# Interleaving a group's last down products with the next pair's first products, with the short weight loads on SyncE's queue, a third short buffer and subtraction for the quads' s4

## The chip, the cores and the metric

The kernel runs on one core of one Trainium2 chip. A core has TensorE (PE; its weight loads are shown as PEld), VectorE (DVE), ScalarE (ACT), GpSimd (POOL), SyncE (SP) and 16 DMA engines. The metric is the device time of one execution in microseconds (us); lower is better. The median of several runs is what counts.

## The reference

A two-layer encoder trunk on 512 tokens plus 16 meta tokens (T = 528 columns, 1024 features, float32). Each layer is a SwiGLU feed-forward net (FFN), a mixer (gated linear attention beside softmax attention) and a second FFN, each with its own RMS norm, added to the residual stream h. The change touches only the FFNs, of which there are four:

```python
def swiglu(x, w_gate, w_up, w_down):
    return (jax.nn.silu(x @ w_gate) * (x @ w_up)) @ w_down
...
    for l in range(DEPTH):
        h = h + 0.5 * swiglu(rmsnorm(h, norm_gains[l, 0]), ...)
        h = h + mixer(rmsnorm(h, norm_gains[l, 1]), ...)
        h = h + 0.5 * swiglu(rmsnorm(h, norm_gains[l, 2]), ...)
    return rmsnorm(h, final_norm)[:, N_META:]
```

The hidden width is 2816, that is 22 tiles of 128.

## The kernel before, in words

**Seven products in place of eight.** Weights and activations are split as 2x2 blocks and multiplied by the scheme of Strassen and Winograd: seven block products and a number of sums, instead of eight products. The products are called "1" to "7" in the code. Products "1", "2" and "4" take a block of the weights as it is (`DIRECT`, L50). "7", "6", "5" and "3" take sums of blocks, called s3, s2, s1 and s4: s3 = w21 - w11, s2 = w22 + s3, s1 = w21 + w22, s4 = s2 - w12.

**Steps of an FFN.** `ffn_steps` (L53) writes the order out by hand. The 22 hidden tiles are 11 pairs; a pair's gate and up weights give seven products, steps ("P", pair, product), done in `product_of_pair` (L549; its matmuls are L566). The pairs fall into groups of 4, 4 and 3 (`GROUPS`, L42). The first two groups are "fast" (`FAST`): their down product is done with the seven-product scheme too, in two halves (0 and 1) of the output rows, steps ("S", group, half, product, part), done in `fast_down` (L663; its matmuls are L680, its adds into h are L688). One such group of seven products of one half is called a quad here. The third group's down product is done plainly, steps "D". Steps "O" make the operands of the fast down product (L630 to L652).

Every step of kind P, and every S step in one piece, is 24 matmuls over 264 columns, or 256 in the last FFN, where the meta tokens are dropped. At a fast group's end the down products come in the order of `zip(AB, "16273465734")` (L75), where `AB` (L48) says which half: half 1's "1", half 0's "6", half 1's "2", half 0's "7", "3", "4", and then half 1's "6", "5", "7", "3", "4". The next group begins with its first pair's "1", "2", "6", "5" (L61, L64).

**Banks.** The results lie in two PSUM pools of two buffers each, "ss" and "s2"; even pairs use s2, odd pairs ss. The last pair of a fast group is odd (3 or 7). Half 1's "1", "6", "7" and "4" sum up in one buffer of ss; after "1", "6" and "7" VectorE adds what is there so far into h (L688) before the next product sums on. Half 1's "5" and "3" share another buffer of ss.

**Weights.** The class `Weights` (L166) loads each block of 128x1024 values (512 KB), and `make` (L245) splits it into two parts for TensorE: a rounded high part on ScalarE (whi, L259) and the low rest on VectorE (wlo, L260). `fetch` (L231) runs up to nine loads ahead, `make` two to three. Buffers:

- raw, 3: the blocks "11", "12" and "22" of the direct products, loaded on SyncE's queue (L193).
- long (`wsa`), 3: s3 and s4.
- short (`wsb`), 2: s2 and s1. Their plain loads go out on POOL's queue (L193, since `pool` is set).
- whi and wlo, 4 each.

`sums` (L205) makes the sums: s3 as a negation of w11 on ScalarE (L198) and an accumulating DMA of w21 (s<-win, L203); s2 as a plain load of w22 and an accumulating DMA of s3 (w<-s, L203); s1 as a plain load of w21 and an accumulating DMA of w22 (w<-win, L203). Accumulating DMAs are issued by POOL alone. s4 is made in one of two ways. For a "late" index (L219: pairs 2 to 10) it is a subtraction on VectorE (L228), s2 minus the kept w12, traced when "6" is made; w12 keeps its raw buffer until then. For the others (pairs 0 and 1, and the quads, which have the indices 11 to 14) it is a negation of w12 on ScalarE and an accumulating DMA of s2 (s<-w), traced when "2" is made.

**Order on the engines.** The program is written as one sequence of operations. A scheduler of the language then fixes the order on each engine and each queue before the run, by priorities and its own estimates of durations; it may move an instruction ahead of others whose inputs it expects later. At run time each engine and queue works through its own list.

The pools `wsa` and `wsb` are opened in `block_pools` (L1091).

Of the kernel before, what the change touches and what calls it, by code (L numbers as in the profile page):

```python
# [17 lines left out]
P = 128  # L18
# [24 lines left out]
FAST = 2  # L43
# [4 lines left out]
AB = (1, 0, 1, 0, 0, 0, 1, 1, 1, 1, 1)  # L48
# [4 lines left out]
def ffn_steps(opening):  # L53

    steps, pair = [], 0
    for g, n in enumerate(GROUPS):

        ahead = g == 0  # L60
        steps += [("P", p, c) for p in range(pair, pair + 1 + ahead) for c in "12"]  # L61
        early4 = (0, 1) if opening and ahead else ()
        steps += [("P", p, "4") for p in early4]
        steps += [("P", pair, c) for c in "65"]  # L64
        for i in range(n):
            p, more = pair + i, i + 1 < n
            early = [[("P", p + 1, "1")], [("P", p + 1, "2")]] if more else \
                [[("D", g, 0, 0, 2 * n - 2)], [("D", g, 1, 0, 2 * n - 2)]]
            if ahead and i == 0:
                early = [[], []]  # L70
            if not more and g < FAST:
                rest = [("S", g, 0, c, 2) for c in "125"]
                steps += [("O", g, 0), ("P", p, "7"), ("P", p, "4"), ("S", g, 0, "1", 1), ("P", p, "3")]
                steps += [("S", g, 0, c, 1) for c in "25"] + [("O", g, 1)] + rest
                steps += [("S", g, *t, 3) for t in zip(AB, "16273465734")]  # L75
                continue
            steps += early[0] + [("P", p, "7")] + early[1] + [("P", p, c) for c in "43" if c == "3" or p not in early4]
            if more:
                steps += [("P", p + 1, "6"), ("P", p + 1, "5")]
        if g >= FAST:  # L80
            steps += [("D", g, m, 0, 2 * n - 2) for m in range(2, HELD)]
            steps += [("D", g, m, 2 * n - 2, 2 * n) for m in range(HELD)]
            steps += [("D", g, m, 0, 2 * n) for m in range(HELD, KC)]
        pair += n
    return steps


def weight_plan():
# [8 lines left out]
    def ffn(l, f):  # L97
        for step in ffn_steps((l, f) == (0, 0)):
            if step[0] == "P":
                plan.append(("op", (l, f)) + step[1:])  # L100
            elif step[0] == "S":
                if step[4] != 2:
                    plan.append(("op", (l, f), NPAIR + QUADS * step[1] + step[2], step[3]))
            elif step[0] == "D":
                _, g, m, first, last = step
                mat("ffn_w_down", (l, f), m * P, 2 * sum(GROUPS[:g]) + first, last - first)
# [37 lines left out]
NPAIR = FF // P // 2  # L144
# [21 lines left out]
class Weights:  # L166
# [21 lines left out]
    def block(self, f, i, name, pool=None, tag="raw"):  # L188

        w = (pool or self.raw).tile([P, SLAB], F32, tag=tag, name=f"w{name}_{f[0]}{f[1]}_{i}")  # L190
        first = f + (i, name) == (0, 0, 0, "11")
        for a in np.split(np.arange(SLAB), 2 if first else 1):
            (self.nc.gpsimd if pool else self.nc.sync).dma_start(w[:, a[0] : a[-1] + 1], self.dram(f, i, name)[:, a[0] : a[-1] + 1])  # L193
        return w

    def negative(self, f, i, name, w):
# [8 lines left out]
    def sums(self, f, i, product, w):  # L205


        got = self.summed
        if product == "1":
            s3 = self.negative(f, i, "s3", w)  # L210
            self.add(s3, self.dram(f, i, "21"))
            s2 = self.block(f, i, "22", self.short, "wsb")
            self.add(s2, s3)
            got[f, i, "7"], got[f, i, "6"] = s3, s2
        if product == "12"[(f, i) in OPENING]:
            s1 = self.block(f, i, "21", self.short, "wsb")
            self.add(s1, self.dram(f, i, "22"))
            got[f, i, "5"] = s1
        late = 2 <= i < NPAIR  # L219
        if product == "2" and not late:  # L220
            s4 = self.negative(f, i, "s4", w)
            self.add(s4, got[f, i, "6"])
            got[f, i, "3"] = s4
        if product == "2" and late:
            self.kept = w
        if product == "6" and late:
            s4 = self.long.tile([P, SLAB], F32, tag="wsa", name=f"s4_{f[0]}{f[1]}_{i}")
            self.nc.vector.tensor_tensor(s4, w, self.kept, ALU.subtract)  # L228
            got[f, i, "3"] = s4
# [67 lines left out]
def build(tc, ctx, xt, wts, win, par, w2, const, umask, out):  # L297
    nc = tc.nc
    V, S, G, TE = nc.vector, nc.scalar, nc.gpsimd, nc.tensor
# [15 lines left out]
    def open_pools(side, psum=(), **bufs):  # L315
        made[0] += 1
        out = {}
        for n, b in bufs.items():
            space = dict(space=bass.MemoryType.PSUM) if n in psum else dict(side=side)
            out[n] = tc.alloc_tile_pool(name=f"{n}_{made[0]}", bufs=b, reuse_waits="tile", **space)  # L320
        slots.update(out)
        return out
# [218 lines left out]
    def ffn(l, f, norm, done, following):  # L541

        x, rs, up, n = norm.x, None, None, live[0]
        w = n // 2
        pools = open_pools("left", psum=("s2",), c=4, s2=2)
        made, hid, sums, raw, sets = {}, {}, {}, {}, {}
        risen = iter(range(KC))

# [144 lines left out]
        def down(g, m, first, last):  # L693
# [16 lines left out]
            if g == len(GROUPS) - 1:  # L710
                lower_h(m, rs)
                (done or finish_chunk)(m)

        steps = ffn_steps((l, f) == (0, 0))
        last_op = max(i for i, t in enumerate(steps) if t[0] == "P")
        for i, step in enumerate(steps):
# [372 lines left out]
        norm.pools = open_pools("right", **{"x": dict(x=16), "xc": dict(xc=8)}[kind])  # L1089

    def block_pools():  # L1091
        pools = open_pools("left", wsa=3, wsb=2)
        W.long, W.short = pools["wsa"], pools["wsb"]
        return pools

# [89 lines left out]
    def finish_chunk(c):  # L1185
        fin.square(c)
        gain(c, slice(0, SEQ))

    def ending(sums, operand, rs):

        table("abs_reciprocal_sqrt_and_small")
# [44 lines left out]
    first = Norm(G_NORM)  # L1236
    operand_pools(first, "xc")
    bp = [block_pools()]
    nc.sync.dma_start(h(1), xt[:, 1])
    first.pair(0)  # L1240
# [15 lines left out]
    for l in range(DEPTH):  # L1256
        a, b, c = norms[3 * l : 3 * l + 3]
        ffn(l, 0, a, b.chunk, lambda: operand_pools(b, "x"))
        close_pools(bp.pop())
        mixer(l, b, c.chunk_of_pair, lambda: (operand_pools(c, "xc"), bp.append(block_pools())))  # L1260
        if l < DEPTH - 1:
            d = norms[3 * l + 3]
            ffn(l, 1, c, d.pair_of, lambda: operand_pools(d, "xc"))
        else:
            ffn(l, 1, c, None, lambda: None)
# [72 lines left out]
```

## Time and profile before

| | |
|---|---|
| median of 3 runs | 2267.75 us (2262.52 to 2270.09) |
| the profiled execution's own time | 2280.39 us |
| its span, first to last instruction | 2278.6 us |
| mean granted TensorE clock | 0.989 |
| TensorE busy | 2188.9 us |
| VectorE, ScalarE, GpSimd busy | 1685.8, 1262.7, 246.1 us |
| moved by DMA | 338.68 MB |

How it is read: busy times of the engines overlap. A row of the grouped views gives the line of the code, the engine, the operation, output and inputs by the program's names (w, s and raw are weight blocks, ss and s2 PSUM buffers, both shown as ss; c and g hold activations), the count, the busy time and mean, and the idle time just before with what ended it. In a timeline row the first number is the start in us from the span's start, the second the duration; an entry in brackets is the idle time of that engine just before, and what ended it. Views of windows give, for a stretch of time, the busy time of each engine, the mean granted clock (PEclk, 1.00 is full), the mean busy share of the 16 DMA engines and the GB/s moved.

### The profile page before, as it was taken

To read this page: it belongs to the slowest core of one execution; us is meant where nothing else is said; L and a number is where in the kernel's file an instruction comes from. 1 tells how busy PE (TensorE), PEld (TensorE's weight loads), DVE (VectorE), ACT (ScalarE), POOL (GpSimd) and SP (SyncE) were. 2 spreads that over 40 slices of the span, in tenths; PEclk is the share of its full clock that TensorE was granted. 3 is DMA by queue.
4 is the path that set the end of the run, shared out by engine and by line. 5 is a ranking of instruction groups with operands and counts; after the bars stand their busy time and mean duration, and the time that the engine had idled before them with its cause. 6 is when DMAs were issued, how large, how long until landed. Compare 5 with 4: busy or idle time off the path is not lost.

```text
span 2278.6 us, 40100 instructions
## 1 busy us (share of the span) xinstructions
PE 2188.9 (96%) x16506; PEld 2088.3 (92%) x16506; DVE 1685.8 (74%) x2607; ACT 1262.7 (55%) x1831; POOL 246.1 (11%) x328
## 2 busy tenths in 40 slices
PE   6989999999999999999999899999999999999998
PEld 6989999989999999998999898998888888999997
DVE  7776867586886678667788768575878767786867
ACT  7545545354785565454575455454547846555553
POOL 1211110000000011111012111100000001121110
PEclk9999999999999999999999999999999999999999
DMA  8877873212113477777668777832121135887871
GB/s 241 217 198 185 203 195 106 77 54 66 47 38 112 129 189 187 204 192 202 175 148 208 201 193 178 201 114 86 56 74 47 47 121 136 216 213 213 204 204 65
DMA packets 94951, 338.68 MB, mean 149 GB/s; under 512 B 10544, under 2 KB 12976, under 8 KB 94768
## 3 DMA queue, kind: packets, MB, share of 16 engines
q0 software_dynamic: 46656, 169.89, 33.9%
q1 hardware_dynamic: 46160, 163.73, 21.2%
q8 instruction: 130, 2.13, 0.4%
q10 hardware_dynamic: 1952, 2.50, 0.3%
q14 instruction: 53, 0.43, 0.1%
HBM read 289.94 MB, written 2.10 MB: 128 GB/s over the span
## 4 chain that ended last, share of the span: by engine, by line
PE 60%; DMA 13%; DVE 12%; issue 8%; ACT 6%; POOL 1%; SPq 0%; DVEq 0%; POOLq 0%; ACTq 0%
PE ss L566 24%; PE mm L433 14%; DMA w<-win 10%; PE ss L433 9%; PE ss L680 4%; DVE wlo L260 3%; PE sm L433 2%; DMA w<-s 2%; ACT whi L259 1%; PE sm L1041 1%; DMA s<-w 1%; PE ss L1016 1%; POOL w L203 1%; ACT s L198 1%; PE sm L1057 1%
## 5 line engine op out<-in xcount | busy, mean ns | idle before, releaser
L566 PE MATMUL ss<-xc,whi 128*128 128x264 f32 (+1 forms) x4928 | 905.6, 285 | 25.6 <-ACT whi L259 13.4
L566 PEld LDWEIGHTS ss<-xc,whi 128*128 128x128 f32 x4928 | 767.1, 189 | 30.8 <-ACT whi L259 14.3
L566 PE MATMUL ss<-xc,wlo 128*128 128x264 f32 (+1 forms) x2464 | 702.1, 285 | 3.7 <-DVE wlo L260 3.7
L260 DVE TENSOR_TENSOR wlo<-w,whi 128x1024 fp32r<-128x1024 f32 (+1 forms) x301 | 365.5, 1217 | 155.6 <-ACT whi L259 155.4
L566 PEld LDWEIGHTS ss<-xc,wlo 128*128 128x128 f32 x2464 | 466.3, 189 | 5.8 <-DVE wlo L260 5.8
L259 ACT CAST whi<-w 128x1024 fp32r<-128x1024 f32 (+1 forms) x301 | 313.0, 1047 | 143.1 <-DMA w<-win 34.0
L433 PE MATMUL mm<-x,whi 128*128 128x264 f32 (+1 forms) x1712 | 385.3, 315 | 0.0
L433 PEld LDWEIGHTS mm<-x,whi 128*128 128x128 f32 x1712 | 279.2, 189 | 16.5 <-issue 1.0
L680 PE MATMUL ss<-g,whi 128*128 128x264 f32 (+1 forms) x1280 | 250.9, 294 | 29.2 <-DVE h L688 17.2
L433 PE MATMUL mm<-x,wlo 128*128 128x264 f32 (+1 forms) x856 | 266.7, 316 | 0.0
L680 PEld LDWEIGHTS ss<-g,whi 128*128 128x128 f32 x1280 | 206.8, 196 | 35.9 <-ACT whi L259 19.5
L259 ACT CAST whi<-raw 128x1024 fp32r<-128x1024 f32 x126 | 132.1, 1049 | 164.4 <-PE mm L433 103.0
L570 ACT COPY c<-ss 128x528 f32<-128x528 f32 (+1 forms) x132 | 78.5, 595 | 224.3 <-PE ss L566 224.1
L260 DVE TENSOR_TENSOR wlo<-raw,whi 128x1024 fp32r<-128x1024 f32 x126 | 153.9, 1222 | 59.3 <-ACT whi L259 58.5
L680 PE MATMUL ss<-g,wlo 128*128 128x264 f32 (+1 forms) x640 | 186.1, 291 | 0.7 <-DVE wlo L260 0.7
L193 POOL DMA_DIRECT2D w<-win x120 | 69.1, 576 | 1079.9 <-DVE x L422 731.2
L260 DVE TENSOR_TENSOR wlo<-s,whi 128x1024 fp32r<-128x1024 f32 x120 | 146.5, 1221 | 43.5 <-ACT whi L259 43.4
L433 PEld LDWEIGHTS mm<-x,wlo 128*128 128x128 f32 x856 | 160.1, 189 | 8.5 <-issue 0.7
L433 PE MATMUL ss<-g,whi 128*128 128x264 f32 (+2 forms) x900 | 166.2, 299 | 0.0
L259 ACT CAST whi<-s 128x1024 fp32r<-128x1024 f32 x120 | 126.1, 1051 | 22.7 <-PE ss L680 15.3
L433 PEld LDWEIGHTS ss<-g,whi 128*128 128x128 f32 x900 | 131.7, 188 | 5.3
L680 PEld LDWEIGHTS ss<-g,wlo 128*128 128x128 f32 x640 | 125.3, 196 | 1.0 <-DVE wlo L260 1.0
(266 smaller groups left out, 3430.8 us busy)
## 6 DMA issues: line engine op xcount, KB each, us to landing
w<-win POOLq DMA_DIRECT2D x180, 512.0 KB, 6.1
w<-win SPq DMA_DIRECT2D x179, 512.0 KB, 5.4
raw<-wts SPq DMA_DIRECT2D x126, 512.0 KB, 3.3
s<-win POOLq DMA_DIRECT2D x60, 512.0 KB, 7.6
w<-s POOLq DMA_DIRECT2D x60, 512.0 KB, 5.2
s<-w POOLq DMA_DIRECT2D x24, 512.0 KB, 7.7
h<-xt SPq DMA_DIRECT2D x3, 528.0 KB, 8.7
out<-h ACTq DMA_DIRECT2D x4, 256.0 KB, 2.3
```

What stands on the lines that cost most here:

```text
L193: (self.nc.gpsimd if pool else self.nc.sync).dma_start(w[:, a[0] : a[-1] + 1], self.dram(f, i, name)[:, a[0] : a[-1] + 1])
L198: self.nc.scalar.activation(t, w, AF.Copy, scale=-1.0)
L203: self.nc.gpsimd.dma_start(t, src, accum_op=ALU.add)
L259: nc.scalar.copy(hi[:, cs], w[:, cs])
L260: nc.vector.tensor_tensor(lo[:, cs], w[:, cs], hi[:, cs].bitcast(F32), ALU.subtract)
L433: TE.matmul(acc.half[i][:width], lhs, rhs[:, acc.spans[i]], start=first, stop=last)
L566: TE.matmul(acc[:, j], a[:, j, k], b[:, at], start=bool(begin and k == 0 and i == 0), stop=k == len(x) - 1 and i == 2, skip_group_check=no ...
L570: W.behind = S.copy(part(st, q), acc).ins
L680: TE.matmul(acc[:, j], a[:, j, k], xs[b][:, k], start=bool(begin and k == 0 and i == 0), stop=k == 3 and i == 2, skip_group_check=not begin)
L1016: TE.matmul(s[:n, i, :HF], lhs, kh[:, hs], start=True, stop=False)
L1041: TE.transpose(tp[:, j * w + u * n : j * w + (u + 1) * n], pr[:n, (2 * c2 + j) * P : (2 * c2 + j + 1) * P], ident[:n, :n])
L1057: TE.matmul(o[:, :w], vw, ph, start=i == 0, stop=False)
```

## The change

1. **Turns.** The last five down products of a fast group, half 1's "6", "5", "7", "3" and "4", take turns with the next group's first pair's "1", "2", "6" and "5": "6", pair "1", "5", pair "2", "7", pair "6", "3", pair "5", "4". The next group no longer begins with these four (`begun`). The plan of the weights follows the same list, so their loads and splits change their order with it.
2. **Queue.** All plain loads of `block` are issued by SyncE, the 120 of the short blocks too, which POOL issued before. POOL keeps the accumulating DMAs.
3. **Third short buffer.** `wsb` has 3 buffers in place of 2.
4. **s4 of the quads.** `late` now holds for every index from 2 on, so the 16 quads' s4 are subtractions on VectorE in place of a negation on ScalarE and an accumulating DMA. w12 of a quad keeps its raw buffer until then.

```diff
@@ ffn_steps @@
         ahead = g == 0
-        steps += [("P", p, c) for p in range(pair, pair + 1 + ahead) for c in "12"]
+        begun = 0 < g <= FAST
+        steps += [("P", p, c) for p in range(pair, pair + 1 + ahead) for c in "12"] * (not begun)
...
-        steps += [("P", pair, c) for c in "65"]
+        steps += [("P", pair, c) for c in "65"] * (not begun)
...
-                steps += [("S", g, *t, 3) for t in zip(AB, "16273465734")]
+                turns = [("S", g, *t, 3) for t in zip(AB, "16273465734")]
+                steps += turns[:6]
+                for s, c in zip(turns[6:], "1265"):
+                    steps += [s, ("P", p + 1, c)]
+                steps.append(turns[-1])
                 continue
@@ Weights.block @@
-            (self.nc.gpsimd if pool else self.nc.sync).dma_start(w[:, a[0] : a[-1] + 1], self.dram(f, i, name)[:, a[0] : a[-1] + 1])
+            self.nc.sync.dma_start(w[:, a[0] : a[-1] + 1], self.dram(f, i, name)[:, a[0] : a[-1] + 1])
@@ Weights.sums @@
-        late = 2 <= i < NPAIR
+        late = 2 <= i
@@ block_pools @@
-        pools = open_pools("left", wsa=3, wsb=2)
+        pools = open_pools("left", wsa=3, wsb=3)
```

## The prediction

> **What bounds the kernel now.** I read the page first, then TensorE's waits, then the windows around its longest pauses, then VectorE and the queues inside one of them.
>
> ```profile
> PE 2188.9 (96%) x16506; PEld 2088.3 (92%) x16506; DVE 1685.8 (74%) x2607; ACT 1262.7 (55%) x1831; POOL 246.1 (11%) x328
> ```
> TensorE is busy for 96% of the span, and the change neither adds nor removes a matmul. So it can only win back pauses, or make new ones. The view of TensorE's waits has one large entry among the down products (line 680):
> ```profile
> PE ss L680 <- DVE h L688: 18.5, 8, 4.3
> ```
> All of its long pauses stand ahead of one step, the last down product of a group (half 1's "4"). There are eight such places: four FFNs with two fast groups each. Here is each from the end of the product ahead of it to the start of the next pair's first product (columns: stretch, its length, busy time of PE, PEld, DVE, ACT, POOL, granted clock, DMA share, GB/s):
> ```profile
> 154.34:164.00 9.66, 5.37 (x26) 5.24 (x25) 4.73 (x5) 1.05 (x1) 0.56 (x1) 0.65 0.96 236
> 289.94:296.84 6.90, 4.69 (x26) 4.56 (x25) 4.72 (x5) 1.04 (x1) 0.56 (x1) 0.75 1.02 223
> 927.03:934.55 7.52, 4.42 (x26) 4.29 (x25) 4.73 (x5) 1.85 (x2) 1.42 (x2) 0.81 1.00 247
> 1061.90:1068.94 7.04, 4.67 (x26) 4.55 (x25) 4.72 (x5) 1.04 (x1) 0.85 (x2) 0.76 1.03 265
> 1297.36:1304.30 6.94, 4.68 (x27) 4.55 (x25) 4.72 (x5) 1.05 (x1) 0.56 (x1) 0.75 0.96 219
> 1434.06:1441.57 7.51, 4.56 (x26) 4.44 (x25) 4.72 (x5) 1.04 (x1) 0.57 (x1) 0.77 0.96 207
> 2044.12:2046.95 2.83, 2.83 (x27) 2.83 (x26) 1.99 (x2) 1.05 (x1) 0.75 (x1) 1.00 0.96 233
> 2170.36:2173.18 2.82, 2.82 (x26) 2.82 (x25) 1.99 (x2) 1.05 (x1) 0.54 (x1) 1.00 1.01 231
> ```
> The stretch needs the time of 24 matmuls. The last two, in the last FFN with 256 columns, take just that. With 264 columns the pitch comes from TensorE's timeline, at the start of half 1's "7":
> ```profile
> 148.48 0.41 PE L680 MATMUL ss<-g,whi 128*128 128x264 f32 x2
> 148.73 0.28 PE L680 MATMUL ss<-g,wlo 128*128 128x264 f32 x1
> 148.85 0.41 PE L680 MATMUL ss<-g,whi 128*128 128x264 f32 x2
> ```
> Three matmuls start in 0.366 us, so 24 take 2.93. The six long stretches add up to 45.57 us; less 6 x 2.93 = 17.58, **28.0 us are lost there**. The waits row holds 18.5 us of it as idle time; the other 9.5, 1.6 us a place, is the product itself running slowly after the pause, at mean granted clocks of 0.65 to 0.81.
>
> Why does VectorE add half 1's "7" into h so late? Its timeline in the same place, and in the last FFN:
> ```profile
> 149.68 1.23 DVE L260 TENSOR_TENSOR wlo<-w,whi 128x1024 fp32r<-128x1024 f32 x1 [0.30 <-ACT whi L259]
> 156.80 1.23 DVE L228 TENSOR_TENSOR s<-w,w 128x1024 f32<-128x1024 f32 x1 [5.89 <-DMA w<-s]
> 157.94 0.70 DVE L688 TENSOR_TENSOR h<-h,ss 128x528 f32<-128x528 f32 x1
> ```
> ```profile
> 2041.49 0.69 DVE L688 TENSOR_TENSOR h<-h,ss 128x512 f32<-128x512 f32 x1 [0.60 <-PE ss L680]
> 2044.96 1.23 DVE L228 TENSOR_TENSOR s<-w,w 128x1024 f32<-128x1024 f32 x1 [2.78 <-DMA w<-s]
> ```
> VectorE sits idle for 5.89 us with the finished product's add behind the waiting instruction: it works its queue in order. In the first six places the subtraction of line 228, which makes the next pair's s4, stands ahead of the add of line 688, and itself waits for an accumulating DMA (w<-s, s2 += s3). "4" sums into the bank that this add must read first. In the last FFN the add comes first; the subtraction still waits 2.78 us, and TensorE loses nothing. So the price is the blocked add, not the late weight, which pair 4 needs only three products later.
>
> **The change part by part.**
>
> *The turns.* The next pair's "1", "2", "6" and "5" now stand between half 1's last five products. Between "7" and "4", which share a bank, lie three products instead of one: 8.8 us instead of 2.9 for the add, so a wait of up to 5.9 us more is covered. It also moves the load of the pair's first block one place ahead of half 1's last block. The chain that makes s2 in the present order (POOL's, ScalarE's, SyncE's and VectorE's timelines):
> ```profile
> 142.33 0.87 POOL L203 DMA_DIRECT2D s<-win  x1 [7.91 <-ACT s L198]
> 143.49 1.18 POOL L193 DMA_DIRECT2D w<-win  x2 [0.30 <-issue]
> 149.99 0.89 POOL L203 DMA_DIRECT2D w<-s  x1 [5.33 <-DMA w<-win]
> ```
> ```profile
> 152.82 1.03 ACT L259 CAST whi<-w 128x1024 fp32r<-128x1024 f32 x1
> ```
> ```profile
> 133.18 0.33 SPq L193 DMA_DIRECT2D w<-win  x1
> ```
> ```profile
> 137.12 0.33 SPq L193 DMA_DIRECT2D w<-win  x1
> ```
> ```profile
> 117.16 1.22 DVE L260 TENSOR_TENSOR wlo<-w,whi 128x1024 fp32r<-128x1024 f32 x1
> ...
> 129.95 1.22 DVE L260 TENSOR_TENSOR wlo<-s,whi 128x1024 fp32r<-128x1024 f32 x1
> ```
> Today: load at 133.18, then the negation, which POOL waits for; s3 is summed from 142.33 (7.6 us), s2 from 149.99 (6.8 us), there at 156.8. In the new order I estimate: the block takes the raw buffer that half 1's "1" leaves at 117.16 + 1.22 = 118.4; the negation waits for the long buffer that half 0's "7" leaves at 129.95 + 1.22 = 131.2; then 1.1 (the negation, its mean is below) + 7.6 + 6.8 and half a microsecond of issue give about 147. Half 1's "7" starts at 148.48 today; with the pair's "1" and "2" ahead of it, 2 x 2.93 later, at 154.3, and the pair's "6" at 157.3. So the subtraction may stand anywhere in VectorE's queue from 147 on without holding anyone. I take 25 of the 28.0 us; the ends are 28.0 and 0.
>
> *SyncE's queue.* All 120 plain short loads leave POOL for SP.
> ```profile
> L193 POOL DMA_DIRECT2D w<-win x120 | 69.1, 576 | 1079.9 <-DVE x L422 731.2 <-DVE wlo L260 167.0 <-issue 65.7
> ```
> ```profile
> w<-win POOLq DMA_DIRECT2D x180, 512.0 KB, 6.1
> w<-win SPq DMA_DIRECT2D x179, 512.0 KB, 5.4
> ```
> POOL saves 69.1 us that nobody waited for; SP gains 120 x 0.33 = 40 us over the whole span, also free. What counts is what stands behind a waiting instruction: on POOL a short load without a buffer held the accumulations; on SP it will hold the raw loads. Cover: the load issued at 137.12 is cast at 152.82, that is 15.7 us less 5.4 for landing, 10.3 us of lead. I cost it at 0; beyond that lead each microsecond would reach TensorE.
> The Trainium skill ("DMA: Bandwidth & Descriptors", section "Issuing engines are not separate DMA queues") says that DMAs from all issuing engines run on the same 16 DMA engines and interleave, so that the issuer saves only issue time. By that rule this part is worth 0 as well; the same two landing times, 6.1 and 5.4 us, lie close.
>
> *Third short buffer.* In the opening, s2 of pair 1 could be loaded only after a short buffer came free:
> ```profile
> 37.77 1.18 POOL L193 DMA_DIRECT2D w<-win  x2 [6.30 <-DVE t L471]
> 45.08 0.90 POOL L203 DMA_DIRECT2D w<-s  x1 [6.13 <-DMA w<-win]
> ```
> ```profile
> 47.36:57.30 9.94, 5.96 (x26) 5.50 (x25) 6.19 (x8) 3.53 (x4) 2.78 (x4) 0.69 1.05 186
> ```
> TensorE's pause there ends with this sum's cast: 9.94 - 2.93 = 7.0 us lost. With a third buffer the block is there early and the sum starts some 6 us sooner. DMA share is 1.05, so not all of it comes back: I take 4, ends 7.0 and -3 (the raw loads now queue behind the short ones at the start).
>
> *s4 of the down quads by subtraction.* 16 negations on ScalarE and 16 accumulating DMAs go; 16 subtractions on VectorE come, of 1.22 us by the row of 156.80 above (1.23 there), 19.5 us. ScalarE's row, and VectorE where the two of a group fall:
> ```profile
> L198 ACT ACTIVATE s<-w 128x1024 f32<-128x1024 f32 x84 | 88.6, 1057 | 66.9 <-DMA w<-win 55.1 <-DVE wlo L260 11.5
> ```
> ```profile
> 108.00:116.00 8.00, 8.00 (x68) 8.00 (x67) 4.10 (x8) 5.54 (x7) 2.30 (x3) 1.00 0.96 212
> ...
> 132.00:140.00 8.00, 7.35 (x59) 6.92 (x57) 6.99 (x8) 4.11 (x5) 0.86 (x1) 1.00 0.83 181
> 140.00:148.00 8.00, 7.98 (x65) 7.98 (x66) 7.67 (x8) 4.11 (x4) 1.98 (x3) 1.00 0.76 188
> ```
> Half 0's has room: VectorE is busy 4.10 of 8 us when its operands are there. Half 1's falls into the stretch with 1.34 us free in 16. I take 0 for the first and half a microsecond for each of the other eight: 4 us, ends 0 and 19.5. Removed accumulations only free DMA time.
>
> **Sum.** 25 + 4 - 4 = 25 us less: the profiled execution's 2280.39 becomes 2255.4. That execution lies 12.6 us above the median of the runs, 2267.75; the median becomes **2243 us**.
>
> **The rivals.**
>
> *Half of it (2257).* VectorE's order is fixed ahead of time, and nothing I read shows it for the new program. If the subtraction still stands ahead of the add by more than the 5.9 us of new cover in some groups, half of the 28.0 us stays: 2267.75 - 14 + 4 - 1 is 2257. For it: the waits of line 228 in six of eight places. Against: the chain starts some 15 us sooner.
>
> *No change (2268).* The DMA engines set the pace: the share is 0.96 to 1.03 in all eight windows, and shorter pauses only make the next weights late. Then 25 us of pause come back as waits of casts for DMA. Against: the last two windows have the same share and no loss. The rule of the Trainium skill named above would support this rival as far as the queue move goes.
>
> *Slower (2277): the blocked add moves to the quads.* The new subtractions also read an accumulated s2.
> ```profile
> DVE s L228 <- DMA w<-s: 39.5, 12, 5.9
> ```
> Today 12 of these subtractions wait, 3.3 us each and 5.9 at most. If half 1's does so in the stretch where VectorE has 0.7 us to spare per 8, each costs 3.3 - 0.7 plus 1.6 of slow clock, 4.2; eight make 34, against 25 gained: 2267.75 + 9 = 2277, and 2290 if they wait 5 us. It decides from a mean wait of 2.2 us on: 8 x (2.2 - 0.7 + 1.6) = 25. Against: s2 of half 1 is there by about 131 (its accumulation is a landing of 6.8 after a load long before), and its long buffer comes free only at 132.9.
>
> **How the numbers follow.** Forecast 0.55, with an own range of 2230 to 2256; half of it 0.12; no change 0.12; slower 0.21. A measurement of this kernel tells about 0.3%, 6.8 us, from no change: below 2261 is faster (0.55 + 0.12 = 0.67), up to 2274.6 the same (0.12), above slower (0.21). The range runs from 2228 (the whole 28.0 and 7.0 us and a few more) to 2288, past the slower case's middle; about 0.05 lies below and 0.12 above.
>
> **What would show it.** Right: the eight windows ahead of half 1's "4", now filled by the pair's "6" and "5", show granted clock 1.00 and no pause over 0.5 us; the wait of L680 for DVE L688 falls from 18.5 to a few us; L228 has 52 instructions; POOL issues no plain load. The opening's pause of 3.5 us shrinks. Wrong: L228 waits for w<-s inside the quads, SP waits over 10 us for a short buffer with casts waiting behind it, or the 28 us reappear as casts waiting for w<-win.

## The result, and the profile after

The changed kernel takes **2235.25 us**, the median of four runs (2233.24 to 2235.91). The kernel before took 2267.18 us in the four runs beside it. The ratio is **0.986, with a 95% interval of 0.9842 to 0.9878**: 32 us less, where 25 were forecast. The profiled execution of the changed kernel ran 2233.24 us, with a span of 2231.4 us. Lines of the kernel behind the changed list of steps now have a number higher by 5 (566 is 571, 680 is 685, 688 is 693, 228 is 233, 198 is 203, 259 and 260 are 264 and 265). In the traces of the experiments they shift again by the lines that an edit adds.

The first part of the page after:
```profile
span 2231.4 us, 40120 instructions
...
PE 2170.3 (97%) x16506; PEld 2075.3 (93%) x16506; DVE 1700.7 (76%) x2623; ACT 1244.2 (56%) x1815; POOL 164.4 (7%) x192
```
TensorE runs the same 16506 matmuls. Its busy time is 18.6 us shorter, though no matmul was taken away: before, matmuls after a pause ran slowly. The rest of the 47.2 us between the two profiled spans is idle time.

TensorE's waits in the trace after (what it waited for: us in all, times, longest):
```profile
PE ss L571 <- ACT c L575: 16.5, 11, 4.8
PE ss L685 <- DVE c L647: 9.4, 14, 0.9
...
PE ss L685 <- DVE h L693: 3.1, 2, 1.6
```
The wait of the down products for VectorE's add was 18.5 us and is 3.1. At the top now stands another one, a gate or up product that waits for ScalarE's snapshot (line 575), with 4.8 us at the longest.

The eight stretches of half 1's "4" in the trace after, in the columns that the prediction used:
```profile
156.00:158.90 2.90, 2.90 (x26) 2.90 (x25) 1.22 (x1) 1.05 (x1) 0.00 (x0) 1.00 1.02 281
282.82:285.76 2.94, 2.94 (x26) 2.94 (x25) 1.27 (x2) 1.05 (x1) 0.00 (x0) 1.00 1.05 268
912.73:915.69 2.96, 2.96 (x27) 2.96 (x26) 1.27 (x2) 1.05 (x1) 0.00 (x0) 1.00 1.05 262
...
2004.15:2006.96 2.81, 2.81 (x26) 2.81 (x25) 1.45 (x2) 1.05 (x1) 0.00 (x0) 1.00 1.05 257
```
All eight look like these: length and busy time are the same, the granted clock is 1.00, and the DMA engines are as full as before (1.02 to 1.05). VectorE's timeline in the first of them:
```profile
142.46 0.70 DVE L693 TENSOR_TENSOR h<-h,ss 128x528 f32<-128x528 f32 x1
...
145.23 1.22 DVE L233 TENSOR_TENSOR s<-w,w 128x1024 f32<-128x1024 f32 x1
146.37 1.22 DVE L265 TENSOR_TENSOR wlo<-w,whi 128x1024 fp32r<-128x1024 f32 x1
147.50 0.70 DVE L693 TENSOR_TENSOR h<-h,ss 128x528 f32<-128x528 f32 x1
```
The subtraction that makes s4 (line 233) still stands ahead of an add, but it waits for nothing: VectorE goes from one row to the next. It is so in all eight places.

The queues and the transfers that were moved, in the page after:
```profile
q1 hardware_dynamic: 63440, 226.65, 28.2%
q0 software_dynamic: 27072, 98.58, 24.4%
...
w<-win SPq DMA_DIRECT2D x299, 512.0 KB, 5.4
s<-win POOLq DMA_DIRECT2D x60, 512.0 KB, 5.2
w<-s POOLq DMA_DIRECT2D x60, 512.0 KB, 5.5
w<-win POOLq DMA_DIRECT2D x60, 512.0 KB, 7.5
s<-w POOLq DMA_DIRECT2D x8, 512.0 KB, 8.4
```
POOL's queue (q0) holds accumulations alone. Its s<-w fell from 24 to 8, the 16 that the quads' subtractions replace.

### The profile page after: what moved, and what is told of

Same layout as the page of the kernel before. It is cut to its first block, busy times and chain, and to the rows that moved or that the text cites. A ratio compares the mean times of both kernels' runs of the same rounds, so it can differ in the third digit from the quotient of the medians.

```text
span 2231.4 us, 40120 instructions
## 1 busy us (share of the span) xinstructions
PE 2170.3 (97%) x16506; PEld 2075.3 (93%) x16506; DVE 1700.7 (76%) x2623; ACT 1244.2 (56%) x1815; POOL 164.4 (7%) x192
## 3 DMA queue, kind: packets, MB, share of 16 engines
q1 hardware_dynamic: 63440, 226.65, 28.2%
q0 software_dynamic: 27072, 98.58, 24.4%
## 5 line engine op out<-in xcount | busy, mean ns | idle before, releaser
L571 PE MATMUL ss<-xc,whi 128*128 128x264 f32 (+1 forms) x4928 | 909.2, 286 | 26.1 <-ACT c L575 16.5
L571 PEld LDWEIGHTS ss<-xc,whi 128*128 128x128 f32 x4928 | 768.8, 190 | 31.1 <-ACT c L575 18.8
L685 PE MATMUL ss<-g,whi 128*128 128x264 f32 (+1 forms) x1280 | 239.5, 285 | 4.4 <-DVE h L693 3.1
L685 PEld LDWEIGHTS ss<-g,whi 128*128 128x128 f32 x1280 | 198.6, 188 | 7.0 <-ACT whi L264 3.4
L685 PE MATMUL ss<-g,wlo 128*128 128x264 f32 (+1 forms) x640 | 181.2, 283 | 0.0
L438 PEld LDWEIGHTS ss<-g,whi 128*128 128x128 f32 x900 | 131.7, 188 | 5.3
L264 ACT CAST whi<-s 128x1024 fp32r<-128x1024 f32 x120 | 126.1, 1051 | 10.9 <-PE ss L571 7.2
L208 POOL DMA_DIRECT2D w<-win x60 | 54.5, 908 | 1029.3 <-DVE wlo L265 410.3
L203 ACT ACTIVATE s<-w 128x1024 f32<-128x1024 f32 x68 | 71.6, 1056 | 89.7 <-DMA w<-win 77.9
```

The source lines that it names most:

```text
L203: self.nc.scalar.activation(t, w, AF.Copy, scale=-1.0)
L208: self.nc.gpsimd.dma_start(t, src, accum_op=ALU.add)
L264: nc.scalar.copy(hi[:, cs], w[:, cs])
L438: TE.matmul(acc.half[i][:width], lhs, rhs[:, acc.spans[i]], start=first, stop=last)
L571: TE.matmul(acc[:, j], a[:, j, k], b[:, at], start=bool(begin and k == 0 and i == 0), stop=k == len(x) - 1 and i == 2, skip_group_check=no ...
L685: TE.matmul(acc[:, j], a[:, j, k], xs[b][:, k], start=bool(begin and k == 0 and i == 0), stop=k == 3 and i == 2, skip_group_check=not begin)
```

## The experiments

My theory at the start: the loss is the add of half 1's "7", held on VectorE by a subtraction that waits for a DMA. The first rival: the DMA engines set the pace, and a pause closed here opens elsewhere. The second, after the result: the turns are not what frees the add. Runs of each part alone and of the change without one part come after these, and then a loss that the trace after shows.

To compare places I took the starts of the matmuls of each product from every trace: wherever more than 0.14 us passes from one start to the next, the excess counts as time lost by TensorE, idle and slow together. The gap ahead of a product and its own slow running stand under that product's name. The limit lies a little above the pitch of 0.122 us (0.366 us for three matmuls), so slow stretches come out a little too small. Worked out so, the loss ahead of half 1's "4" is 25.9 us in the profile before; beyond the pitch itself it is 27.8, against the 28.0 of the prediction's windows. The opening is that of the first FFN, and its pair 3's "4" is counted there. Times are us; the ratios are against the kernel before, run on the same chip beside them.

| run | ratio [95%] | span | lost ahead of half 1's "4" | next pair's first four | half 0's "1" | half 0's "6" | pairs 3 and 7's "4" | opening (pairs 0 to 3) | all places |
|---|---|---|---|---|---|---|---|---|---|
| before, profile shown | | 2278.6 | 25.9 | 0.4 | 10.8 | 13.6 | 7.2 | 18.5 | 106.6 |
| e4_before_again | | 2262.3 | 16.0 | 0.5 | 13.7 | 11.7 | 7.0 | 16.3 | 92.6 |
| after | 0.986 [0.9842, 0.9878] | 2231.4 | 0 | 0 | 5.8 | 16.3 | 14.3 | 12.9 | 65.1 |
| e1_turns_only | 0.9911 [0.9875, 0.9948] | 2259.5 | 0 | 15.2 | 14.8 | 12.2 | 6.8 | 15.5 | 88.7 |
| e2_no_turns | 0.9883 [0.9855, 0.991] | 2249.1 | 0 | 6.0 | 7.6 | 17.4 | 15.2 | 13.5 | 80.9 |
| e3_gated | 0.9913 [0.9882, 0.9945] | 2239.9 | 0 | 0 | 12.4 | 11.8 | 6.1 | 18.8 | 72.4 |
| e5_late_only | 0.9953 [0.9927, 0.9979] | 2259.9 | 0 | 5.2 | 12.6 | 14.5 | 6.7 | 18.1 | 89.0 |
| e6_third_only | 0.9908 [0.988, 0.9937] | 2243.0 | 0 | 0.3 | 15.1 | 11.6 | 10.7 | 16.1 | 75.1 |
| e7_queue_only | 0.9929 [0.99, 0.9957] | 2250.8 | 10.9 | 0 | 15.9 | 11.8 | 11.1 | 12.6 | 82.7 |
| e8_later_negation | 0.9753 [0.9706, 0.98] | 2212.1 | 0 | 0 | 0.9 | 11.2 | 5.1 | 14.4 | 46.3 |
| e9_later_no_turns | 0.9785 [0.9754, 0.9815] | 2221.2 | 0 | 4.0 | 2.3 | 11.2 | 5.4 | 14.5 | 54.8 |
| e10_later_alone | 1.008 [1.0051, 1.0109] | 2291.8 | 32.4 | 0.3 | 16.5 | 9.0 | 5.1 | 17.9 | 119.7 |
| e11_no_queue | 0.9898 [0.9873, 0.9924] | 2245.7 | 0 | 0 | 11.8 | 17.4 | 13.5 | 16.2 | 77.0 |
| e12_no_late | 0.9866 [0.9821, 0.991] | 2240.0 | 0 | 0 | 13.2 | 12.6 | 15.1 | 13.1 | 72.9 |

Span less the last column is 2165.8 to 2172.1 in every row. So these places hold the difference between any two of the kernels up to 6.3 us. The span and the losses belong to the profiled execution, the ratios to medians; the two need not rank alike (e3_gated).

**e1_turns_only.** The kernel before with the new list of steps alone:
```diff
+        begun = 0 < g <= FAST
...
+                turns = [("S", g, *t, 3) for t in zip(AB, "16273465734")]
+                steps += turns[:6]
+                for s, c in zip(turns[6:], "1265"):
+                    steps += [s, ("P", p + 1, c)]
+                steps.append(turns[-1])
```


> Before, with the turns alone (POOL's queue, two short buffers and the quads' s4 by accumulating DMA as before). Blocked add (my theory): three products instead of one lie between half 1's 7 and 4, so the 28 us ahead of 4 mostly go: 2240 to 2248 us. Rival, the DMA pace or the late weight itself: the pauses only move to casts that wait for DMA, 2262 to 2270 us. Rival, the queue and the buffer are what gains: no gain from this part, 2265 us.

Measured: 2258.71 us, 0.9911, more than the 2240 to 2248 of my theory. The loss ahead of "4" is gone, and 15.2 us stand ahead of the pair's first four products instead, which start earlier while their weights do not. TensorE's waits in this trace:
```profile
PE ss L571 <- ACT whi L264: 16.1, 10, 9.3
```
The opening's four waits, 11.2 us, are in this row too; 4.4 us of it stand ahead of the pair's "6", which needs s2. The rest of the 15.2 us, all of it in "6", are waits for the split behind that cast, and slow running. Alone, the turns exchange a blocked add for late casts.

**e2_no_turns.** The changed kernel with the list of steps as before.

> The changed kernel without the turns: SyncE's queue, third short buffer and subtraction for the quads' s4, in the old order of products. Blocked add: the subtraction for the next pair still stands ahead of the add of half 1's 7, so 20 us or more of the 28 stay; only the opening gains some 5 us: 2255 to 2265 us. Rival, queue and buffer are what gains: 2238 to 2245 us.

Measured: 2247.58 us, 0.9883. I had expected 2255 to 2265; this one missed. Without the turns nothing is lost ahead of "4" either. VectorE's timeline in the first place shows why:
```profile
143.16 0.70 DVE L688 TENSOR_TENSOR h<-h,ss 128x528 f32<-128x528 f32 x1 [0.70 <-PE ss L680]
...
150.53 1.23 DVE L228 TENSOR_TENSOR s<-w,w 128x1024 f32<-128x1024 f32 x1 [6.67 <-DMA w<-s]
151.67 1.22 DVE L260 TENSOR_TENSOR wlo<-w,whi 128x1024 fp32r<-128x1024 f32 x1
```
```profile
152.94 0.39 PE L566 MATMUL ss<-xc,wlo 128*128 128x264 f32 x1 [0.79 <-DVE wlo L260]
```
The subtraction still waits 6.67 us for its sum, but in this program the add of half 1's "7" stands ahead of it, in all eight places. What stands behind it now is the split of the next pair's "2" (151.67), whose cast was done by 144.1: TensorE's first matmul that reads this wlo waits for it. So the 6.0 us in the table are the same fault once more, with a split in the place of the add.

**e3_gated.** The kernel before with one edge of order and nothing else: the subtraction is put behind the add of half 1's "7".
```diff
-            self.nc.vector.tensor_tensor(s4, w, self.kept, ALU.subtract)
+            with self.tc.issue_after(self.gate) if self.gate else nullcontext():
+                self.nc.vector.tensor_tensor(s4, w, self.kept, ALU.subtract)
...
-                V.tensor_tensor(to, to, acc, ALU.add)
+                added = V.tensor_tensor(to, to, acc, ALU.add).ins
+                if (dq, c) == (1, "7"):
+                    W.gate = added
```


> Before, with one order edge on VectorE and nothing else: the subtraction that makes a next pair's s4 may not stand ahead of the add of half 1's 7. Blocked add: the six long pauses ahead of 4 shrink to under 1 us each although the weight comes no earlier, 2240 to 2246 us. Rival, the weight itself or the DMA pace: the same 28 us are lost a few products later, 2262 to 2270 us.

Measured: 2253.89 us, 0.9913; I had expected 2240 to 2246, and the profiled execution, at 2241.63, is the fastest of the five. Here are VectorE's timeline and the windows of two of the eight places in its trace:
```profile
151.17 0.70 DVE L690 TENSOR_TENSOR h<-h,ss 128x528 f32<-128x528 f32 x1 [0.70 <-PE ss L682]
...
154.30 1.23 DVE L230 TENSOR_TENSOR s<-w,w 128x1024 f32<-128x1024 f32 x1 [2.42 <-DMA w<-s]
```
```profile
153.90:156.83 2.93, 2.93 (x26) 2.93 (x25) 2.53 (x3) 1.06 (x2) 0.33 (x1) 1.00 1.04 267
281.97:284.91 2.94, 2.94 (x26) 2.94 (x25) 2.44 (x3) 1.05 (x1) 0.00 (x0) 1.00 1.04 248
```
No DMA, buffer or step differs from before, the DMA share is 1.04, and the loss is 0 in all eight places, nor does it come back in the pair's first four products. So it was the order on VectorE that cost the time, and not the DMA engines. The first rival falls.

**e4_before_again.** The kernel before, profiled a second time.

> The kernel before once more, for a second profile. Its first profiled execution lay 12.6 us above the median of its runs. If that is chance of one execution, this one shows 2262 to 2270 us with the six pauses ahead of 4 at 4 to 5 us each as before and the difference elsewhere; if the profile itself costs it, again about 2280 us.

Measured: 2264.06 us, a span of 2262.3. The time is as expected, the pauses are not: the loss ahead of "4" is 16.0 us where the first profile has 25.9. TensorE's wait for the add (L680 for DVE L688) is 14.1 us instead of 18.5, and the product behind it runs below full clock in two of the six places instead of all six. The first profile is of an execution 12.6 us above the median, so the forecast's 28.0 was too large for the median; two profiles do not tell by how much. Three of its eight windows:
```profile
151.26:157.92 6.66, 4.46 (x27) 4.33 (x26) 4.73 (x5) 1.04 (x1) 0.81 (x2) 0.78 1.01 242
287.49:292.91 5.42, 3.15 (x26) 3.03 (x25) 4.73 (x5) 1.50 (x2) 0.86 (x1) 1.00 1.03 238
924.64:930.19 5.55, 3.17 (x27) 3.05 (x25) 4.73 (x5) 1.04 (x1) 0.00 (x0) 1.00 1.01 230
```

**e5_late_only, e6_third_only, e7_queue_only.** The kernel before with one line of the change each:
```diff
-        late = 2 <= i < NPAIR
+        late = 2 <= i
```


> Before, with the quads' s4 by subtraction alone. The kernel without turns gained 1.2% and lost nothing ahead of half 1's 4, against my expectation; one of its three parts must have taken the subtraction from ahead of the add. Theory: it is this part, since s4 of half 1 no longer takes a long buffer and a POOL slot early, so the next pair's chain runs earlier and ScalarE has two operations less where the group's operands are made: ratio 0.988 to 0.993, pauses at half 0's 1 (part 2) down by half, no pause ahead of 4. Rival, the queue or the buffer did it: ratio 0.997 to 1.003 with 16 us or more still lost ahead of 4.


```diff
-        pools = open_pools("left", wsa=3, wsb=2)
+        pools = open_pools("left", wsa=3, wsb=3)
```


> Before, with the third short buffer alone. My term for it: the opening gains 4 us (3 to 6), nothing else; ratio 0.996 to 0.999, 16 us or more still lost ahead of 4. Rival, the buffer moves the next pair's sum so far ahead that the subtraction no longer blocks: ratio 0.988 to 0.992.


```diff
-            (self.nc.gpsimd if pool else self.nc.sync).dma_start(w[:, a[0] : a[-1] + 1], self.dram(f, i, name)[:, a[0] : a[-1] + 1])
+            self.nc.sync.dma_start(w[:, a[0] : a[-1] + 1], self.dram(f, i, name)[:, a[0] : a[-1] + 1])
```


> Before, with the short loads on SyncE's queue alone. My term for it: 0; ratio 0.997 to 1.003, 16 us or more still lost ahead of 4. By the rule that the issuer saves only issue time, the same. Rival, accumulating DMAs no longer stand behind plain loads on POOL and land sooner, and the subtraction no longer waits: ratio 0.988 to 0.993 with landing of w<-s clearly under 5.2 us. Rival on the other side, raw loads wait behind short ones: ratio over 1.003.

Measured: 2260.58 (0.9953), 2250.89 (0.9908) and 2254.67 us (0.9929). The first is a smaller gain than I expected; the other two are larger than my terms of the sum and lie in the ranges of their rivals. The subtraction's wait for its sum in each of the three traces, in that order:
```profile
DVE s L228 <- DMA w<-s: 50.2, 9, 6.9
```
```profile
DVE s L228 <- DMA w<-s: 4.3, 5, 1.3
```
```profile
DVE s L228 <- DMA w<-s: 29.1, 12, 3.8
```
The third buffer makes the sum arrive in time, so that the subtraction hardly waits wherever it stands. VectorE's timeline of e6_third_only shows the old order, without the wait:
```profile
148.52 1.23 DVE L228 TENSOR_TENSOR s<-w,w 128x1024 f32<-128x1024 f32 x1
149.66 0.70 DVE L688 TENSOR_TENSOR h<-h,ss 128x528 f32<-128x528 f32 x1
```
The quads' subtractions alone leave the sum late (50.2 us of waits), but in the new program the adds no longer stand behind it; the 5.2 us ahead of the next pair's products are again the split of its "2". The queue alone shortens the waits, and 10.9 of 16 to 25.9 us remain ahead of "4".

**e8_later_negation, e9_later_no_turns, e10_later_alone.** The trace after shows a loss that I had not foreseen. In the last FFN, pair 3, ScalarE's timeline and then TensorE's:
```profile
1935.81 0.83 ACT L646 CAST g<-g 128x768 fp32r<-128x768 f32 x1
1942.97 1.06 ACT L203 ACTIVATE s<-w 128x1024 f32<-128x1024 f32 x1 [6.33 <-DMA w<-win]
1943.93 0.81 ACT L646 CAST c<-g 128x768 fp32r<-128x768 f32 x1
1944.66 0.58 ACT L575 COPY c<-ss 128x512 f32<-128x512 f32 x1
```
```profile
1945.29 0.50 PE L571 MATMUL ss<-xc,whi 128*128 128x256 f32 x2 [4.84 <-ACT c L575]
```
It is the same fault on another engine. The negation that makes s3 waits 6.33 us for its load, and the snapshot for which TensorE waits stands behind it. The edit, on the changed kernel, sums the blocks of "1" four steps later and puts the negation behind the latest snapshot:
```diff
-                    self.sums(*load, self.raws[self.fetched])
+                    self.waiting.append((self.fetched, load, self.raws[self.fetched]))
...
+        while self.waiting and self.waiting[0][0] <= j + 5:
+            _, load, w = self.waiting.pop(0)
+            self.sums(*load, w)
...
-        self.nc.scalar.activation(t, w, AF.Copy, scale=-1.0)
+        with self.tc.issue_after(self.behind) if self.behind else nullcontext():
+            self.nc.scalar.activation(t, w, AF.Copy, scale=-1.0)
```


> The changed kernel, with the sums of a pair's or quad's first block traced four steps later and s3's negation ordered behind the latest snapshot on ScalarE. In the last FFN of the changed kernel a negation that waits for its load stands ahead of a snapshot, and TensorE loses some 12 us at the last product 4 of both groups and just behind it that it did not lose before. If that blocked snapshot is the cause, those 12 us go: 2223 to 2227 us if nothing else moves. Rival, the later start of s3 makes the sums late, and casts wait for DMA: 2240 us or more.

The same without the turns:

> The kernel of the later negation, without the turns. If the turns are worth what the change with and without them differs by (2235 against 2248 us on other runs, 0.2 to 0.6%), this one takes 2217 to 2226 us. If the turns give the later sums the time that they now need, pauses come back ahead of the next pair's first products: 2230 us or more. If the turns are worth nothing beside the rest: 2210 to 2214 us.

And the same edit on the kernel before:

> Before, with the later negation alone. If a negation that waits for its load holds ScalarE's other work, the pauses at half 0's 1 (part 2, 13.7 us) and at product 2 and 5 shrink; the next pair's s2 comes later, so what is lost ahead of half 1's 4 stays at 16 us or grows: 2245 to 2262 us. Rival, the later negation by itself does most of what the whole change does: 2235 us or less.

Measured: **e8_later_negation takes 2212.55 us (2212.14 to 2213.9), 0.9753, the fastest kernel here**, 24 us under the changed kernel by the ratios and better than the 2223 to 2227 that I expected. ScalarE's timeline at that place now has the snapshot first:
```profile
1936.13 0.59 ACT L579 COPY c<-ss 128x512 f32<-128x512 f32 x1 [1.29 <-PE ss L575]
1936.61 1.05 ACT L265 CAST whi<-s 128x1024 fp32r<-128x1024 f32 x1
1938.69 1.06 ACT L204 ACTIVATE s<-w 128x1024 f32<-128x1024 f32 x1 [1.02 <-DMA w<-win]
```
Against the trace after, 9.2 us went from pairs 3 and 7's "4", 5.1 from half 0's "6" and 4.9 from its "1": 19.2 us together, while the sums of all places differ by 18.8 (the opening loses 1.5 more). Which of the edit's two halves does it was not tried: the snapshot's wait at that place is gone, but the later sums move other work on ScalarE as well.

Without the turns it is 2221.14 us, 0.9785, as expected. On the kernel before, the same edit is *slower*, 2289.43 us, 1.008. I had forecast a larger loss ahead of "4" there, and it is 32.4 us, but the total of 2245 to 2262 missed. Two rows of e10_later_alone's waits:
```profile
PE ss L684 <- DVE h L692: 24.5, 8, 4.2
...
DVE s L229 <- DMA w<-s: 66.9, 20, 5.7
```
A later negation makes s2 later, and with the old program VectorE's adds stand behind the subtraction that waits for s2 (66.9 us of waits, 39.5 before).

**e11_no_queue, e12_no_late.** The changed kernel, with the short loads on POOL again, and with the quads' s4 by negation and accumulating DMA again.

> The changed kernel with the short loads back on POOL's queue (turns, third buffer and subtraction kept). My term for the queue in this company: 0, so 2233 to 2238 us. Rival, the queue is worth the 0.7% that it gave alone: 2246 to 2255 us, with the opening 3 to 4 us longer and accumulating DMAs landing later.

> The changed kernel with the quads' s4 made by negation and accumulating DMA as before (turns, queue and third buffer kept). My term for the subtractions: they cost 4 us, so this one is faster, 2229 to 2233 us. Rival, the two operations less on ScalarE are worth more than the subtractions cost: 2240 to 2250 us, with the pauses at half 0's 1 (part 2) back at 10 us or more instead of 3.4.

Measured: 2246.08 us (0.9898) and 2241.08 us (0.9866). The queue is worth about 9 us in company by the ratios (0.0038 x 2268) and 11 by the medians, where I had 0; the intervals overlap by 0.0005, the runs of the two kernels do not. The subtractions are worth 1 us by the ratios and 6 by the medians; the intervals overlap widely, so their sign in company stays open; a cost of 4 us is not seen, and alone (e5_late_only) they gain 0.5%, clear of 1. ScalarE's waits in the trace of e12_no_late, and then the rows of the same two waits in the trace after:
```profile
ACT s L203 <- DMA w<-win: 95.7, 26, 7.7
...
ACT whi L264 <- DMA w<-win: 38.6, 13, 4.5
```
```profile
ACT s L203 <- DMA w<-win: 77.9, 18, 6.3
...
ACT whi L264 <- DMA w<-win: 5.8, 4, 2.2
```
With the quads' negations and accumulations back, weights are later at ScalarE, and half 0's "1" loses 13.2 us instead of 5.8; half 0's "6" loses 3.7 less.

## Why the prediction was right, and where it failed

**What bounds the kernel** was right. TensorE's pauses are all there is to win (span less lost time is constant within 7 us), and the blocked add is shown by e3_gated: one edge of order removes the loss, with every DMA as before. The no-change rival is refuted by the same run. But "All of its long pauses stand ahead of one step" holds only for the row of waits quoted there: half 0's products (listed under the sum below) lose 39.0 us in the same profile and 35.9 in the second, more than half 1's "4", and the prediction did not look at them.

**The turns: "I take 25 of the 28.0 us". This is the step that failed.** The loss (25.9 or 16.0 us) did go, but it is not the turns' own: each of the turns, the third buffer and the quads' subtractions takes all of it away alone, as does everything but the turns (e2_no_turns). They are redundant: alone the four parts save 0.9, 0.9, 0.7 and 0.5%, 3.0% if they added up, and together 1.4%. My chain of times for the new order (s2 at 147) came out in the changed kernel, whose subtraction starts at 145.23 without a wait; with the turns alone s2 is late, and the pair's "6" waits for its cast. The third buffer, which I had read only in the opening, makes s2 early in the groups too. What the turns are worth beside the others is about 5 us by the ratios (0.9883 against 0.986; these intervals overlap, the runs of the two kernels do not), and 7 beside the later negation (0.9785 against 0.9753; again the intervals overlap and the runs do not). In both pairs the loss that they remove is the next pair's first four products, 6.0 and 4.0 us, and some of half 0's "1". This is the mechanism that I forecast, at a smaller price: without the turns the subtraction waits 50.6 us in 8 places and the split of "2" stands behind it (e2_no_turns), with them it waits for nothing.

**SyncE's queue: "I cost it at 0".** Mis-sized: 0.7% alone, some 9 us in company. My reason, and with it the sentence on the Trainium skill ("DMA: Bandwidth & Descriptors", section "Issuing engines are not separate DMA queues"), looked at what the issuer spends and at one landing time. The runs differ, and the measurement decides. Why, they leave open. The transfers that make s3 landed in 7.6 us before:
```profile
s<-win POOLq DMA_DIRECT2D x60, 512.0 KB, 7.6
```
They land in 5.2 us in the changed kernel, but that is all four parts: 6.7 with the queue alone, 6.3 with all but the queue. The sign that I had named for the rival, w<-s clearly under 5.2 us, did not come: with the queue alone it is 6.2. POOL did hold accumulations behind short loads that waited for a buffer:
```profile
POOL w L193 <- DVE wlo L260: 167.0, 36, 23.3
```
That these waits are what the move takes away is likely, but it was argued, not shown; a landing time counts from the issue and does not hold them. What shows is ScalarE's waits for blocks (whi for w<-win, plain loads and the sums s1 together): 34.0 us before and 9.2 with the queue alone, 35.5 in e11_no_queue and 5.8 in the changed kernel. So nothing shows the cost that the prediction feared, raw loads late behind short ones.

**Third short buffer, 4 us in the opening.** The two profiles have 18.5 and 12.9 us there, but the gain is not the buffer's: with the loads on POOL the opening loses 15.5 to 18.8 us with two buffers, 16.1 and 16.2 with three (e6_third_only, e11_no_queue); with the loads on SP it loses 12.6 (e7_queue_only, two buffers) to 14.5. The pause of 7.0 us that the prediction read is gone with the third buffer alone, and with the queue alone, but it was no fixed price: in the second profile of the kernel before it is 0.8. The buffer's own gain lies in the groups, where I gave it nothing.

**Subtractions for the quads, 4 us of cost.** Not seen, as above: VectorE had the room, and with fewer operations on ScalarE and the DMA engines half 0's "1" loses 5.8 us instead of 13.2 (against e12_no_late), while half 0's "6" loses 3.7 more.

**The sum.** 25 us forecast and 32 measured lie close by luck; the terms compensate: the loss ahead of "4" is 16 to 26 us for all parts together, half 0's products ("1", "4", "6" and the first parts of "2" and "5") lose 22.3 us instead of 35.9 to 39.0, which I had not counted at all, and pairs 3 and 7's "4" give 7 us back (7.2 to 14.3) through the negation on ScalarE, which I did not foresee. The rival "half of it" has a slip in its sum: by the prediction's own terms (14 and 4 us less, 4 more) it is 2254 us, not 2257. The "slower" rival, subtractions that wait inside the quads, did not come. In the groups of the trace after, line 233 has 52 instructions and 0.1 us of idle time ahead of them in all:
```profile
L233 DVE TENSOR_TENSOR s<-w,w 128x1024 f32<-128x1024 f32 x52 | 63.4, 1219 | 0.1
```

## What to carry to other kernels

On an engine that works in order, look at what stands *behind* an instruction that waits for a DMA; one edge of order that moved that instruction gave 0.9% here, where buffers, queues and a new order of the work gave 1.4% together. Parts of a change that relieve the same wait are not to be added up, and each part is to be read in every stage that it touches: try each alone and all but it. After one such block is gone, look for the next on another engine; the same edit that gains 1% then can cost 0.8% earlier (e8_later_negation and e10_later_alone).

## What the runs showed of the hardware that I had not expected

Accumulating DMAs took twice the DMA engines' time per byte. By the queue rows after, 98.58 MB of accumulations took 24.4% of the engines' span (0.248% per MB) and 226.65 MB of plain transfers 28.2% (0.124% per MB), a factor of 1.99. It is the accumulating and not POOL's queue: e7_queue_only moves 62.92 MB of plain loads from POOL's queue to SP's, and POOL's share falls by 7.5 points (33.9 to 26.4%) while SP's rises by 8.5 (21.2 to 29.7%), so plain loads cost about the same on either.

The granted clock after a pause is not set by the pause's length alone. In e4_before_again's three windows above, TensorE is idle for 2.20, 2.27 and 2.38 us (length less busy time); the first has a mean clock of 0.78 and 1.5 us more of busy time than 2.93, the other two 1.00. What else decides can be read in the same trace: the clock is 1.00 or 0.50 there and changes only at times that lie whole multiples of 3.41 us apart. Here are such steps around the first of these pauses, and then the two that share the second:
```profile
151.60:155.01 3.41, 1.39 (x11) 1.42 (x12) 3.38 (x4) 1.04 (x1) 0.00 (x0) 1.00 0.98 253
155.01:158.42 3.41, 3.41 (x18) 3.41 (x17) 1.61 (x3) 0.00 (x0) 0.55 (x1) 0.50 1.03 249
```
```profile
288.12:291.53 3.41, 1.62 (x13) 1.65 (x14) 3.41 (x5) 0.87 (x1) 0.25 (x1) 1.00 1.08 261
291.53:294.95 3.42, 3.42 (x30) 3.42 (x29) 1.83 (x2) 0.00 (x0) 0.55 (x1) 1.00 0.98 260
```
The first pause puts 2.02 us of idle time into one step, and the next step runs at 0.50. The second leaves 1.79 us in one step and the rest in the step before, and the clock stays. The other four of these pauses go the same way: 2.09 us in one step and the clock falls, 1.62 or less and it stays. So a pause of this length costs 1.3 us more or nothing, by where it falls. This is not the whole rule: steps with 1.5 to 1.9 us idle went either way in this case's traces, and a stretch of the mixer lowers the clock without a long pause (587.0 to 590.4 us in the trace before).

The time also became steadier, for which no cause was tried. The four runs of the kernel before lie within 7.6 us (22 others from 2257.01 to 2289.7), the changed kernel's four within 2.7 and e8_later_negation's four within 1.8.
